# One decoder layer on one core: the order of the first round's loads and products, and the chain of the last norm

## The chip, the core and the metric

The kernel runs on one core of a Trainium2 chip. The core has five engines with queues of their own: PE (matmuls; its weight loads are shown as PEld), DVE and ACT (elementwise work), POOL (GpSimd) and SP, which here only issues DMAs. ACT and POOL can issue DMAs too. The metric is the device time of one execution in microseconds (us), taken as the median of several runs.

## What is computed

The reference is one layer of a decoder trunk in float32 for 256 tokens behind 16 meta tokens, with a width of 2048:

```python
h = jnp.concatenate([meta, x], axis=1)
h = h + hybrid_mixer(rmsnorm(h, norm_mix_g[l]), w_in[l], ...)
h = h + squared_relu_mlp(rmsnorm(h, norm_mlp_g[l]), w_ff1[l], w_ff2[l])
return rmsnorm(h, final_norm_g)[:, N_META:]
```

The mixer projects the normalised input with `w_in` to the operands of a forgetting attention (8 heads) and of a gated linear attention (4 heads), projects both results, gates them and sums them. The MLP is 2048 to 8192 to 2048. What matters here are the two ends: the first products of `w_in` with the input, and the last norm, `rmsnorm(h, final_norm_g)`, with the store of the output.

## The kernel before

**Layout.** Everything is held transposed: `h` has 128 partitions, 16 tiles (`KT`) of 128 channels, 272 tokens, and three columns of gains. A weight block ("chunk") is 2048 x 128, that is 16 tiles of 128 x 128. Each matmul operand is split into a high and a low part (`hi`, `lo`): ACT casts (`whi`), DVE subtracts (`wlo`); the input `x` is split in the same way, with the gain applied. A product is hi x hi, hi x lo and lo x hi. Raw weights, high parts and low parts have five buffers each (`raw`, `whi`, `wlo`). In the main stream SP loads half a chunk (512 KB, line 118), ACT casts it (line 120), DVE makes the low part (line 121), and PE multiplies (lines 136 and 137, or 153 to 155 where all 272 tokens are wanted).

**Order.** The program is written for all engines in one order; a planner that simulates a timeline then sets the order of instructions on each engine (`schedule_with_timeline_sim`). What the planner sets is fixed: an engine does not pass an instruction that waits. `tc.issue_after(ins)` puts what is written in its block behind `ins` on the engine of `ins`.

**First round (lines 259 to 346).** The first seven chunks are not done one after the other but together, so that PE can start before a whole chunk is there. There are eight stages; stage s brings channel tiles k = 2s and 2s+1 of all seven chunks, as one load for chunks 0 to 3 (`wa`, 512 KB) and one for chunks 4 to 6 (`wb`, 384 KB). Stage 0 alone comes in four loads, one for each tile and group. Each chunk accumulates in a PSUM bank of its own (`first_ps`). For each k PE does the high products of all chunks (lines 330, 332, 333) and then the low ones (lines 337, 339). `h` is loaded by line 284: tiles 0 and 1 from ACT's queue, and 2-3, 4-7, 8-15 from SP's queue, between the loads of stages 0, 1 and 2. Lines 317 and 318 make `x`; `square(q)` (lines 288, 290) squares four tiles of `h` for the first norm and is written behind stages 2 to 5. Constants (`cons`), the small columns of `w_in` (`wsm`) and `w_alpha2` follow on SP's queue. Behind the round the seven banks are read out (`total`, lines 162 and 165), the squares are summed over channels by PE (line 208), and PE multiplies the small columns (lines 153 to 155, tile `psa`); it needs a bank that one `total` has set free.

**End (lines 829 to 887).** The last four blocks of `w_ff2` (`NL`) are done in another order: the low products of all 256 tokens first (line 835), and then the high products for tokens 0 to 127 (`half(0, ...)`) and for tokens 128 to 255 (`half(P, ...)`, line 844). Behind each block of a half ACT copies one part of the bank (line 847), DVE adds both to `h` (lines 848, 849), ACT squares (line 851) and applies the gain (line 852), and POOL adds the squares of all but the last block to `acc` (line 854). `root_of` sums the squares over channels on PE (lines 862, 863) and takes the inverse root (`fast_root`, lines 766 to 774: DVE, ACT's square root, a reciprocal, and one Newton step). `spread` puts the roots on a diagonal (line 216, DVE) and has PE spread them over all partitions (line 219). `finish` multiplies `h` and stores it: tokens 0 to 127 on POOL from a copy `r_half` (line 881) with stores from SP's queue, tokens 128 to 255 on DVE straight from PSUM with stores from ACT's queue (lines 871, 872). `finish0`, which does this for the first half, is written behind the third of the second half's four blocks.

Of the kernel before, what the change touches and what calls it, by code (L numbers as in the profile page):

```python
# [16 lines left out]
P = 128  # L17
# [48 lines left out]
def trunk(ctx: ExitStack, tc: tile.TileContext, hT, w_small, w_all, consts, w_alpha2, out):  # L66
# [198 lines left out]
    def first_weights(c0, n, k0):  # L265
# [6 lines left out]
        def load(k, nk):  # L272
            nc.sync.dma_start(r[:, :, k : k + nk, :],
                              w_all[c0 : c0 + n, :, (k0 + k) * P : (k0 + k + nk) * P].rearrange("c p (k m) -> p c k m", m=P))
# [19 lines left out]
    def load_stage(s):  # L294
        stages[s] = [first_weights(c0, n, 2 * s) for c0, n in ((0, 4), (4, 3))]
        for k in range(2) if s == 0 else (0,):
            for hi, lo, load, cut in stages[s]:
                load(k, 1 if s == 0 else 2)

    load_h(nc.scalar, 0, 1)  # L300
    load_h(nc.scalar, 1, 1)
    for _ in range(5):
        nc.tensor.matmul(warm[:, 0:NT], ones[:, 0:P], ones[:, 0:NT], start=True, stop=True)
    load_stage(0)
    load_h(nc.sync, 2, 2)
    load_stage(1)
    load_h(nc.sync, 4, 4)
    load_stage(2)
    load_h(nc.sync, 8, 8)
    nc.sync.dma_start(cons, consts)  # L310
    for s in range(KT // 2):
        if s not in stages:
            load_stage(s)
        wa, wb = stages[s]
        for kk in range(2):
            k = 2 * s + kk
            nc.scalar.activation(x[:, k, 0, :], h[:, k, 0:NA], AF.Identity, scale=gain(0, k))
            nc.vector.scalar_tensor_tensor(x[:, k, 1, :], h[:, k, 0:NA], gain(0, k),
                                           x[:, k, 0, :].bitcast(F32), op0=ALU.mult, op1=ALU.subtract)
            for hi, lo, load, cut in (wa, wb):  # L320
                if s == 0:
                    cut(kk, 1)
                elif kk == 0:
                    cut(0, 2)
            at = [(w[0][:, c, kk, :], w[1][:, c, kk, :]) for w, n in ((wa, 4), (wb, 3)) for c in range(n)]
            st, sp = k == 0, k == KT - 1
            for c, (hi, lo) in enumerate(at):
                ps = first_ps[c]
                if c < NF - 1:
                    nc.tensor.matmul(ps, hi, x[:, k, :, NM:NA], start=st, stop=False)  # L330
                else:
                    nc.tensor.matmul(ps[:, 0:NA], hi, x[:, k, 0, :], start=st, stop=False)
                    nc.tensor.matmul(ps[:, 0:NA], hi, x[:, k, 1, :], start=False, stop=False)
            for c, (hi, lo) in enumerate(at):
                ps = first_ps[c]
                if c < NF - 1:
                    nc.tensor.matmul(ps[:, 0:NT], lo, x[:, k, 0, NM:NA], start=False, stop=sp)  # L337
                else:
                    nc.tensor.matmul(ps[:, 0:NA], lo, x[:, k, 0, :], start=False, stop=sp)
        if s in (2, 3, 4, 5):  # L340
            square(s - 2)
    chunk[0] = NF
    nc.sync.dma_start(wsm, w_small)
    nc.sync.dma_start(wa2[0:16], w_alpha2)
# [419 lines left out]
    def fast_root(sums, n):  # L764
# [7 lines left out]
        nc.vector.tensor_tensor(r, y, y, op=ALU.mult)  # L772
        nc.vector.scalar_tensor_tensor(r, r, -0.5, v, op0=ALU.mult, op1=ALU.mult)
        nc.vector.scalar_tensor_tensor(y, r, 1.5, y, op0=ALU.add, op1=ALU.mult)
        return y
# [63 lines left out]
    def half(t0, between):  # L839

        tok = slice(t0, t0 + P)
        for n, (j, w, ps) in enumerate(ends):
            for k in range(KT):
                nc.tensor.matmul(ps[:, NT:], w(k)[0], a[:, k, :, tok], start=(k == 0), stop=(k == KT - 1))  # L844
            between[n]()
            b = tmp.tile([P, P], F32, tag="evb", name=nm("evb"))
            nc.scalar.copy(b, ps[:, NT + P :])
            nc.vector.tensor_tensor(ht[:, j, tok], ps[:, NT : NT + P], ht[:, j, tok], op=ALU.add)
            nc.vector.tensor_tensor(ht[:, j, tok], ht[:, j, tok], b, op=ALU.add)
            sq = gat.tile([P, P], F32, tag="sq", name=nm("sq"))  # L850
            nc.scalar.activation(sq, ht[:, j, tok], AF.Square)
            nc.scalar.activation(ht[:, j, tok], ht[:, j, tok], AF.Identity, scale=gain(2, j))
            if n < NL - 1:
                nc.gpsimd.tensor_tensor(acc[:, tok], acc[:, tok], sq, op=ALU.add)
        return sq
# [4 lines left out]
    def root_of(i, sq):  # L860
        tok = slice(P * i, P * (i + 1))
        nc.tensor.matmul(pn[i][:, P : P + 1], acc[:, tok], ones[:, 0:1], start=True, stop=False)
        nc.tensor.matmul(pn[i][:, P : P + 1], sq, ones[:, 0:1], start=False, stop=True)
        box[i] = fast_root(pn[i][:, P : P + 1], 1)

    def finish(i, r, pieces):
        tok = slice(P * i, P * (i + 1))
        j0 = 0
        for n, eng in pieces:
            o = ht[:, j0 : j0 + n, tok]  # L870
            eng.tensor_tensor(o, o, r[:, 0:P].unsqueeze(1).to_broadcast([P, n, P]), op=ALU.mult)
            (nc.sync if i == 0 else nc.scalar).dma_start(out[i][:, j0 : j0 + n, :], o)
            j0 += n

    v, p, none = nc.vector, nc.gpsimd, lambda: None
    sq = half(0, [none] * NL)

    def finish0():
        r = gat.tile([P, P], F32, tag="r", name="r_half", bufs=1)
        spread(pn[0], box[0], (0,), P)  # L880
        nc.scalar.copy(r, pn[0][:, 0:P])
        finish(0, r, ((2, p), (2, p), (4, p), (4, p), (4, p)))

    sq = half(P, [lambda: root_of(0, sq)] + [none] * (NL - 3) + [finish0, none])
    root_of(1, sq)
    spread(pn[1], box[1], (0,), P)
    finish(1, pn[1], ((2, v), (2, v), (4, v), (4, v), (4, v)))
# [60 lines left out]
```

## Time and profile before

| | us |
|---|---|
| median of three runs | 1633.47 |
| lowest, highest | 1631.92, 1634.26 |
| the profiled execution's own time | 1630.68 |
| its span in the profile | 1629.0 |
| PE busy in the span | 1609.0 |

The span runs from the first to the last instruction of the profiled execution; 1.68 us of its own time lie around it. PE's busy time is the sum of its matmuls, which are pipelined, and their ends are modelled; here it is used to find the places where PE stands still. A row of a timeline gives start, duration, engine, line, operation, written tile, read tiles, shapes and count; behind it in brackets stand the idle time of the engine just before and what ended it. A row of the chain of waits gives start, duration, engine, tile and line; the chain is followed back from the last instruction.

### The profile page before, as it was taken

How to read it: one execution, taken by the hardware profiler on the slowest of the kernel's cores; microseconds unless marked ns; L12 is line 12 of the kernel's file. 1: busy time of each engine (PE TensorE's matmuls, PEld its weight loads, DVE VectorE, ACT ScalarE, POOL GpSimd, SP SyncE). 2: the span in 40 equal slices, each digit the busy share in tenths (PEclk: the TensorE clock that was granted, in tenths of full speed). 3: DMA queues.
4: the chain of work that ended last, by engine and by line, in shares of the span. 5: the costliest groups of instructions: out<-in, count | busy, mean ns of one | idle time of the engine just before them, and what ended most of it. 6: DMA issues, size and time to landing. Idle time of an engine off the chain costs nothing.

```text
span 1629.0 us, 25617 instructions
## 1 busy us (share of the span) xinstructions
PE 1609.0 (99%) x9996; PEld 1447.2 (89%) x9996; DVE 1033.8 (63%) x1591; ACT 788.3 (48%) x1217; POOL 93.5 (6%) x146
## 2 busy tenths in 40 slices
PE   8999999999999999999999999999999999999997
PEld 7999999999998888888888888888888888888886
DVE  6767657476665555555677776566655676567655
ACT  6555444454445444444555544444444444444553
POOL 1000000010000000000011000000000000000022
PEclk9999999999999999999999999999999999999998
DMA  9444555455555555565555556565566565565552
GB/s 296 137 150 158 159 167 161 164 186 160 161 157 169 191 185 190 186 191 187 188 189 188 185 189 189 187 191 186 181 196 190 188 187 188 188 190 187 190 189 73
DMA packets 90266, 292.97 MB, mean 180 GB/s; under 512 B 9096, under 2 KB 21648, under 8 KB 89888
## 3 DMA queue, kind: packets, MB, share of 16 engines
q1 hardware_dynamic: 87552, 288.88, 55.8%
q8 instruction: 78, 1.28, 0.3%
q10 hardware_dynamic: 2416, 1.33, 0.3%
q0 software_dynamic: 176, 1.12, 0.2%
q14 instruction: 44, 0.36, 0.1%
HBM read 289.19 MB, written 2.11 MB: 179 GB/s over the span
## 4 chain that ended last, share of the span: by engine, by line
PE 97%; DMA 1%; DVE 1%; ACT 0%; issue 0%; SPq 0%; DVEq 0%; ACTq 0%
PE ps L136 50%; PE ps L137 26%; PE psa L155 5%; PE psa L154 5%; PE psa L153 5%; PE ps L844 1%; PE ps L330 1%; DMA h<-hT_dram 1%; PE pa L492 1%; PE ps L835 0%; PE ps L337 0%; PE po L556 0%; DMA raw<-w_all_dram 0%; PE pz L390 0%; PE po L557 0%; PE pq L653 0%
## 5 line engine op out<-in xcount | busy, mean ns | idle before, releaser
L121 DVE TENSOR_TENSOR wlo<-raw,whi 128x1024 fp32r<-128x1024 f32 x522 | 639.9, 1226 | 500.7 <-ACT whi L120 498.9
L120 ACT CAST whi<-raw 128x1024 fp32r<-128x1024 f32 x522 | 548.0, 1050 | 747.5 <-PE ps L136 505.0
L136 PE MATMUL ps<-x,whi 128*128 128x512 f32 x1952 | 685.9, 394 | 0.0
L137 PE MATMUL ps<-x,wlo 128*128 128x256 f32 x1952 | 548.6, 281 | 0.0
L136 PEld LDWEIGHTS ps<-x,whi 128*128 128x128 f32 x1952 | 366.6, 188 | 82.8
L137 PEld LDWEIGHTS ps<-x,wlo 128*128 128x128 f32 x1952 | 367.6, 188 | 0.0
L136 PE MATMUL ps<-a,whi 128*128 128x512 f32 x960 | 335.8, 395 | 0.0
L137 PE MATMUL ps<-a,wlo 128*128 128x256 f32 x960 | 270.0, 282 | 0.0
L136 PEld LDWEIGHTS ps<-a,whi 128*128 128x128 f32 x960 | 180.2, 188 | 40.7
L153 PE MATMUL psa<-x,whi 128*128 128x272 f32 x640 | 186.7, 292 | 2.1 <-DVE ri L196 2.1
L155 PE MATMUL psa<-x,whi 128*128 128x272 f32 x640 | 185.9, 290 | 0.0
L154 PE MATMUL psa<-x,wlo 128*128 128x272 f32 x640 | 184.6, 288 | 0.0
L137 PEld LDWEIGHTS ps<-a,wlo 128*128 128x128 f32 x960 | 181.7, 189 | 0.3
L153 PEld LDWEIGHTS psa<-x,whi 128*128 128x128 f32 x640 | 121.3, 190 | 2.8 <-issue 2.1
L154 PEld LDWEIGHTS psa<-x,wlo 128*128 128x128 f32 x640 | 120.6, 188 | 0.2
L155 PEld LDWEIGHTS psa<-x,whi 128*128 128x128 f32 x640 | 120.3, 188 | 0.1
L136 PE MATMUL ps<-og,whi 128*128 128x512 f32 x256 | 89.9, 393 | 0.0
L136 PE MATMUL ps<-y,whi 128*128 128x512 f32 x256 | 89.1, 392 | 0.0
L756 POOL TENSOR_TENSOR acc<-acc,hsq 128x256 f32<-128x256 f32 x26 | 28.5, 1096 | 774.8 <-ACT hsq L755 774.8
L137 PE MATMUL ps<-y,wlo 128*128 128x256 f32 x256 | 71.8, 281 | 0.0
L137 PE MATMUL ps<-og,wlo 128*128 128x256 f32 x256 | 71.8, 281 | 0.0
L165 DVE TENSOR_TENSOR evt<-ps,evb 128x256 f32<-128x256 f32 x158 | 66.0, 418 | 0.0
(262 smaller groups left out, 1384.9 us busy)
## 6 DMA issues: line engine op xcount, KB each, us to landing
raw<-w_all_dram SPq DMA_DIRECT2D x537, 512.0 KB, 3.9
raw<-w_all_dram SPq DMA_DIRECT2D x7, 384.0 KB, 6.3
h<-hT_dram SPq DMA_DIRECT2D x1, 1100.0 KB, 9.9
negc<-fdram POOLq DMA_DIRECT2D x1, 1088.0 KB, 5.9
out_dram<-h SPq DMA_DIRECT2D x3, 256.0 KB, 2.6
out_dram<-h ACTq DMA_DIRECT2D x3, 256.0 KB, 3.1
h<-hT_dram SPq DMA_DIRECT2D x1, 550.0 KB, 7.3
raw<-w_all_dram SPq DMA_DIRECT2D x2, 256.0 KB, 4.5
```

Source lines behind the costliest of these rows:

```text
L120: nc.scalar.copy(hi[:, k, :], r)
L121: nc.vector.tensor_tensor(lo[:, k, :], r, hi[:, k, :].bitcast(F32), op=ALU.subtract)
L136: nc.tensor.matmul(ps, hi, x, start=first, stop=False)
L137: nc.tensor.matmul(ps[:, 0:NT], lo, x[:, 0, :], start=False, stop=last)
L153: nc.tensor.matmul(ps[:, 0:n], hi, x[:, k, 0, :], start=(k == 0), stop=False)
L154: nc.tensor.matmul(ps[:, 0:n], lo, x[:, k, 0, :], start=False, stop=False)
L155: nc.tensor.matmul(ps[:, 0:n], hi, x[:, k, 1, :], start=False, stop=(k == KT - 1))
L165: nc.vector.tensor_tensor(t, ps[:, 0:NT], b, op=ALU.add)
L330: nc.tensor.matmul(ps, hi, x[:, k, :, NM:NA], start=st, stop=False)
L492: nc.tensor.matmul(dst, k[:, a, :], q[:, a, :], start=(a == 0), stop=(a == 1))
L756: nc.gpsimd.tensor_tensor(acc, acc, sq, op=ALU.add)
L844: nc.tensor.matmul(ps[:, NT:], w(k)[0], a[:, k, :, tok], start=(k == 0), stop=(k == KT - 1))
```

## The change

First round: the loads of `h` all go to SP's queue, two tiles ahead of each stage's weights (one tile at a time in stage 0). Three stages are loaded ahead; in the loop, stage s+3 is loaded, with its `h` behind the first of its two weight loads. `cons`, `wsm` and `w_alpha2` go behind the last weight load of the round. The squares are written behind stages 2, 4, 6 and 7. In the last stage PE finishes one chunk after the other: for each chunk both k, each with its high and low product.

End: both halves of a bank are added to `h` by DVE straight from PSUM, without ACT's copy. POOL adds the squares of two blocks of a half only; the other two are summed by PE. The Newton step has three DVE instructions as before, each with one tensor operand and scalars. ACT makes the diagonal. The first half's `finish0` is put into the second half's last block, ahead of its k = 4, and the matmuls from k = 4 on are put behind its spreading matmul. The second half's stores alternate between ACT's and SP's queue, with pieces of 2, 4, 4, 4 and 2 tiles.

```diff
         def load(k, nk):
-            nc.sync.dma_start(r[:, :, k : k + nk, :],
+            return nc.sync.dma_start(r[:, :, k : k + nk, :],
...
-    def load_stage(s):
-        stages[s] = [first_weights(c0, n, 2 * s) for c0, n in ((0, 4), (4, 3))]
-        for k in range(2) if s == 0 else (0,):
-            for hi, lo, load, cut in stages[s]:
-                load(k, 1 if s == 0 else 2)
-
-    load_h(nc.scalar, 0, 1)
-    load_h(nc.scalar, 1, 1)
+    def load_stage(s, part):
+        c0, n = ((0, 4), (4, 3))[part]
+        w = first_weights(c0, n, 2 * s)
+        stages.setdefault(s, []).append(w)
+        return w[2](0, 2) if s else w[2]
+
+    load_a, load_b = load_stage(0, 0), load_stage(0, 1)
+    for k in range(2):
+        load_h(nc.sync, k, 1)
+        load_a(k, 1)
+        load_b(k, 1)
     for _ in range(5):
         nc.tensor.matmul(warm[:, 0:NT], ones[:, 0:P], ones[:, 0:NT], start=True, stop=True)
-    load_stage(0)
-    load_h(nc.sync, 2, 2)
-    load_stage(1)
-    load_h(nc.sync, 4, 4)
-    load_stage(2)
-    load_h(nc.sync, 8, 8)
-    nc.sync.dma_start(cons, consts)
+    for s in range(1, 3):
+        load_h(nc.sync, 2 * s, 2)
+        load_stage(s, 0)
+        load_stage(s, 1)
     for s in range(KT // 2):
-        if s not in stages:
-            load_stage(s)
+        if s + 3 < KT // 2:
+            with tc.issue_after(load_stage(s + 3, 0).ins):
+                load_h(nc.sync, 2 * s + 6, 2)
+            last = load_stage(s + 3, 1).ins
...
+        if s < KT // 2 - 1:
+            order = [(c, 2 * s + kk, part) for kk in range(2) for part in range(2) for c in range(NF)]
+        else:
+            order = [(c, 2 * s + kk, part) for c in range(NF) for kk in range(2) for part in range(2)]
+        for o in order:
+            products(*o)
+        if s in (2, 4, 6, 7):
+            square((2, 4, 6, 7).index(s))
     chunk[0] = NF
-    nc.sync.dma_start(wsm, w_small)
-    nc.sync.dma_start(wa2[0:16], w_alpha2)
+    with tc.issue_after(last):
+        nc.sync.dma_start(cons, consts)
+        nc.sync.dma_start(wsm, w_small)
+        nc.sync.dma_start(wa2[0:16], w_alpha2)
...
-        nc.vector.tensor_tensor(r, y, y, op=ALU.mult)
-        nc.vector.scalar_tensor_tensor(r, r, -0.5, v, op0=ALU.mult, op1=ALU.mult)
-        nc.vector.scalar_tensor_tensor(y, r, 1.5, y, op0=ALU.add, op1=ALU.mult)
-        return y
+        nc.vector.tensor_scalar(r, y, y, v, op0=ALU.mult, op1=ALU.mult)
+        nc.vector.tensor_scalar(r, r, -0.5, 1.5, op0=ALU.mult, op1=ALU.add)
+        nc.vector.tensor_scalar(q, r, y, None, op0=ALU.mult)
+        return q
...
+                if within and n == NL - 1 and k == 4:
+                    ahead = within()
+                elif not (within and n == NL - 1 and k > 4):
+                    ahead = None
+                with tc.issue_after(ahead) if ahead else nullcontext():
+                    nc.tensor.matmul(ps[:, NT:], w(k)[0], a[:, k, :, tok], start=(k == 0), stop=(k == KT - 1))
             between[n]()
-            b = tmp.tile([P, P], F32, tag="evb", name=nm("evb"))
-            nc.scalar.copy(b, ps[:, NT + P :])
-            nc.vector.tensor_tensor(ht[:, j, tok], ps[:, NT : NT + P], ht[:, j, tok], op=ALU.add)
-            nc.vector.tensor_tensor(ht[:, j, tok], ht[:, j, tok], b, op=ALU.add)
+            for t in (ps[:, NT : NT + P], ps[:, NT + P :]):
+                nc.vector.tensor_tensor(ht[:, j, tok], t, ht[:, j, tok], op=ALU.add)
...
-            if n < NL - 1:
+            if n < NL - 2:
                 nc.gpsimd.tensor_tensor(acc[:, tok], acc[:, tok], sq, op=ALU.add)
-        return sq
+            else:
+                sqs.append(sq)
+        return sqs
...
+        parts = [acc[:, tok], *sqs]
+        for n, part in enumerate(parts):
+            nc.tensor.matmul(pn[i][:, P : P + 1], part, ones[:, 0:1], start=(n == 0), stop=(n == len(parts) - 1))
...
+    def row(i):
+        d = gat.tile([P, P], F32, tag="d", name=nm("d"))
+        nc.scalar.activation(d, ident, AF.Identity, scale=box[i])
+        last = nc.tensor.matmul(pn[i][:, 0:P], ones[:, 0:P], d, start=True, stop=True)
+        r = gat.tile([P, P], F32, tag="r", name=nm("r_half"))
+        nc.scalar.copy(r, pn[i][:, 0:P])
+        return r, last.ins
 
     def finish0():
...
+        r, last = row(0)
+        finish(0, [(j, n, p, r, nc.sync) for j, n in ((0, 2), (2, 2), (4, 4), (8, 4), (12, 4))])
+        return last
+
+    sqs1 = half(P, [lambda: root_of(0, sqs)] + [none] * (NL - 1), finish0)
+    root_of(1, sqs1)
+    row(1)
+    finish(1, [(j, n, v, pn[1], q) for j, n, q in ((0, 2, nc.scalar), (2, 4, nc.sync), (6, 4, nc.scalar),
+                                                  (10, 4, nc.sync), (14, 2, nc.scalar))])
```

More of the change, by code (lines that the diff above doesn't have):

```diff
@@ L1 @@
-from contextlib import ExitStack
+from contextlib import ExitStack, nullcontext
 import concourse.bass as bass
@@ L324, in trunk @@
                     cut(0, 2)
[L325 to L333, printed above, removed]
@@ L875, in trunk @@
     v, p, none = nc.vector, nc.gpsimd, lambda: None
-    sq = half(0, [none] * NL)
-    def finish0():
[L879 to L887, printed above, removed]
+    sqs = half(0, [none] * NL)
```

39 lines of the change are left out of this document (20 added, 19 removed).

## The prediction

> **What bounds the kernel now.** I read the page first, then the rows of waits, then the timelines of the places where PE waits, and last the chain of waits at the end.
>
> ```profile
> PE 1609.0 (99%) x9996; PEld 1447.2 (89%) x9996; DVE 1033.8 (63%) x1591; ACT 788.3 (48%) x1217; POOL 93.5 (6%) x146
> ```
>
> PE is busy for 1609.0 of a span of 1629.0 us, so a change that takes no matmul away can win at most some 20 us, at the places where PE stands still. The timelines of the first 54 us show them:
>
> ```profile
> 1.28 3.87 PE L303 MATMUL warm<-ones 128*128 128x256 f32 x10 [1.28 <-DVE ones L188]
> ...
> 6.63 1.67 PE L330 MATMUL ps<-x,whi 128*128 128x512 f32 x6 [1.48 <-DVE x L318]
> ...
> 8.20 0.94 ACT L317 ACTIVATE x<-h 128x272 fp32r<-128x272 f32 x2 [0.22 <-DMA h<-hT_dram]
> ...
> 10.05 1.76 ACT L278 CAST whi<-raw 128x1024 fp32r<-128x1024 f32 x2
> ...
> 11.70 1.56 PE L330 MATMUL ps<-x,whi 128*128 128x512 f32 x6
> ...
> 16.41 0.94 ACT L317 ACTIVATE x<-h 128x272 fp32r<-128x272 f32 x2 [0.47 <-DMA h<-hT_dram]
> ...
> 21.74 4.18 ACT L278 CAST whi<-raw 128x768 fp32r<-128x768 f32 x5
> ...
> 22.61 0.73 PE L330 MATMUL ps<-x,whi 128*128 128x512 f32 x2 [2.94 <-ACT whi L278]
> ...
> 35.43 1.56 PE L330 MATMUL ps<-x,whi 128*128 128x512 f32 x6
> ...
> 37.91 1.56 PE L330 MATMUL ps<-x,whi 128*128 128x512 f32 x6
> ...
> 50.20 0.29 PE L339 MATMUL ps<-x,wlo 128*128 128x272 f32 x1
> ...
> 52.56 0.42 DVE L165 TENSOR_TENSOR evt<-ps,evb 128x256 f32<-128x256 f32 x1
> ...
> 53.13 0.37 PE L153 MATMUL psa<-x,whi 128*128 128x272 f32 x1 [2.08 <-DVE ri L196]
> ```
>
> One k of the round takes PE 2.48 us (35.43 to 37.91), 16 take 39.7. The round runs from 6.63 to 50.3, 43.7: it loses 4.0 inside. The large wait is 2.94 us at 22.61, for a cast that ACT begins at 21.74. ACT was late because `x` and squares stood ahead of that cast in its order, and these had waited for the load of `h` tiles 8 to 15 (16.41). Ahead of the round PE waits 1.48; behind it 2.08, because DVE reads out the first bank only at 52.56, when the last product is done. With the 1.28 before the first warm-up product these make 8 of the 20 us. The other twelve lie behind the last product, at 1615.37:
>
> ```profile
> 1611.36 4.01 PE ps L844 x33
> ...
> 1615.39 0.27 ACT evb L847
> ...
> 1615.69 0.30 DVE h L848
> ...
> 1616.02 0.78 DVE h L849
> ...
> 1616.88 0.32 ACT sq L851
> ...
> 1617.24 0.40 PE pn L863 x2
> ...
> 1617.66 0.17 DVE rv L766
> ...
> 1617.85 0.21 ACT rq L768
> ...
> 1618.09 0.17 DVE ry L770
> ...
> 1618.29 0.19 DVE rr L772
> ...
> 1618.50 1.11 DVE rr L773
> ...
> 1619.63 1.10 DVE ry L774
> ...
> 1620.76 0.30 DVE diag L216
> ...
> 1621.10 0.81 PE pn L219 x2
> ...
> 1621.94 0.42 DVE h L871
> ```
> ```profile
> 1613.02 0.46 POOL L854 TENSOR_TENSOR acc<-acc,sq 128x128 f32<-128x128 f32 x1 [1.88 <-ACT sq L851]
> 1613.04 0.53 DVE L216 TENSOR_SCALAR diag<-cons,ry 128x128 f32<-128x128 f32 x1
> ...
> 1615.19 0.38 PE L219 MATMUL pn<-diag,ones 128*128 128x128 f32 x2
> ...
> 1615.96 4.76 POOL L871 TENSOR_TENSOR h<-h,r_half 128x256 f32<-128x256 f32 x5 [0.59 <-ACT r_half L881]
> ```
>
> Lines 773 and 774 work on one column and take 1.1 us each, line 849 takes 0.78. All three read two tensors from SBUF, and all three run while POOL does its five multiplications (1615.96 to 1620.72). The reciprocal (ry, 1618.09), also SBUF to SBUF but with one tensor, takes 0.17 there, and rv, which reads PSUM, 0.17. So a two-tensor operation of DVE waits for POOL's current instruction.
>
> **The change, part by part.** All sums are against the profiled execution (1630.68, span 1629.0). The median of the three runs is 2.8 higher; I take the same difference off it.
>
> *First round.* Two bounds. PE's first product cannot come before the five warm-up products end at 5.15: at most 1.48 is won. Stage 1 gives the sharper one. In both versions the 1171 KB of stage 0 (896 of weights, two tiles of `h` of 137.5) and 275 KB of `h` go ahead of its first weights; that `h` landed by 8.20. The next 512 KB take 1.4 us at the rate of that time:
>
> ```profile
> GB/s 0 82 292 335 314 363 361 398 365 426 406 341 352 366 278 316 347 192 0 198 304 247 331 294 371 382 391 303 267 240 237 164 218 52 0 67 276 52 33 215
> ```
>
> (slices of 1.35 us, some 360 GB/s there), so they land at 9.6; today's cast starts at 10.05, straight behind a square that moves away. Cast and start add 0.9: PE begins stage 1 at 10.5, not 11.70. From there the loads bring a stage (1171 KB) in 3.3 us and PE needs 4.96, so the lead grows.
>
> ```profile
> 6.60:50.30 43.70, 40.56 (x240) 35.45 (x241) 29.50 (x41) 27.07 (x41) 3.75 (x4) 1.00 0.83 276
> ```
>
> Over the round DVE (29.50) and ACT (27.07) are busy for 68% and 62% of the time, today crowded into its first half by the early `h`; spread over the stages they keep up with PE. I expect no further wait but 0.1 for low parts. The round ends at 10.5 + 14 x 2.48 + 0.1 = 45.3: **-5.0**. Nothing won (the planner again puts `x` and squares ahead of casts) is one end, -5.5 (1.48 + 4.0) the other. I choose near the good end, as the named load is split and each piece now lies ahead of its own stage.
>
> SP's order: the first `h` moves from ACT's queue to SP's, and the later tiles go behind loads that wait for a free `raw` buffer; who waits for it is `x`, priced among the rivals. `cons`, `wsm` and `w_alpha2` go behind the last load. That one goes out when stage 5's first load has been cut, which needs a `whi` buffer that PE leaves with stage 2 (10.5 + 2 x 4.96 = 20.4): at about 22. The first user (the small columns' cast) needs a buffer of stage 5, free at 35, so these loads have 13 us. The main stream's weights queue behind them on SP; PE needs those only behind the round.
>
> *Last stage by chunk.* The same matmuls in another order: no cost. The first bank is complete 6/7 of 4.96, 4.2 us, ahead of the end, and its sum takes DVE 0.42 (52.56) behind a shorter copy on ACT. Both have that time, so PE goes straight on: **-2.1**. With the sum placed behind the casts of the main stream again, 0.
>
> *The end.* T is the end of the last product (1615.37 now). Start to start: without ACT's copy -0.30. The second addition reads PSUM; no row shows such an operation begun inside one of POOL's. I take 0.30 like the first, as the nearest row (rv, from PSUM beside POOL) is not held: -0.48; held as today, 0. The Newton step keeps three instructions but with one tensor each; I take 0.20 each like the reciprocal, -1.86 for two; held, they cost what they do now. The diagonal on ACT costs 0.40 + 0.04, like line 852's gain on the same shape, against 0.34: +0.10.
>
> ```profile
> L852 ACT ACTIVATE h<-h x8: 401/402/405, 1602.1 to 1617.2; 128x128 f32<-128x128 f32 x8
> ```
>
> The spreading product took 0.81 at half the clock, and 0.38 for the first half, at full clock. It had fallen by 1618.75, 3.4 us behind T:
>
> ```profile
> 1618.75:1619.00 0.25, 0.00 (x0) 0.00 (x0) 0.25 (x1) 0.00 (x0) 0.25 (x1) 0.50 0.07 19
> ```
>
> Now it would begin 3.2 behind T, just before: -0.42; 0 if the fall comes earlier. The Trainium skill's "TensorE: Matmul & The Clock Gate" ("What's actually happening") says that the clock is cut after an idle window of about 3.4 us that runs freely. The 3.4 agrees; by the rule T need not be a window's start, the fall comes at T + 3.4 at the earliest and mostly later, and the -0.42 holds for sure, where by the row alone 0.2 us of margin decide and it may be 0.
>
> The sum is -2.96: DVE's multiplication begins at T + 3.6 in place of T + 6.6. But POOL moves less. The first half's spreading now stands 12 products ahead of T (12 x 0.12 = 1.46); a copy of 0.27 follows, and ACT has a square and a gain of the third block in the way (0 to 0.7): POOL begins about T - 0.75, not T + 0.59, and ends at T + 4.0, behind DVE's start. So its last store (256 KB) falls into the second half's.
>
> ```profile
> 1625.00:1625.50 0.50, 0.00 (x0) 0.00 (x0) 0.00 (x0) 0.00 (x0) 0.00 (x0) 0.50 0.99 297
> 1627.00:1627.50 0.50, 0.00 (x0) 0.00 (x0) 0.00 (x0) 0.00 (x0) 0.00 (x0) 0.50 0.43 130
> ```
>
> The stores end near 1627.3 with all queues full at some 290 GB/s: 256 KB more cost 0 to 0.9, I take 0.6. Two queues do not help, since the DMA engines are full. End: **-2.4**; with all that may be held, +0.4, and without the overlap -3.0.
>
> *PE's additions.* One more pair of sums ahead of T: **+0.1**. The wait put before k = 4: the diagonal of the first half must be there at T - 1.7. Today it is done at 1613.57 (T - 1.8), 0.2 of it DVE's wait for POOL. If it is late, PE stalls with 12 products behind it: 0 to 1; I take 0.
>
> **Sum:** -5.0 - 2.1 - 2.4 + 0.1 = -9.4: span 1619.6, 1621.3 for this execution, and 1633.5 - 9.4 = **1624.1** for the median.
>
> **The rivals.** *A. The start gives back.* The planner orders ACT and DVE by its own times, and an order that was wrong by several us made today's 2.94. One of the two gains goes: if the readout of the first bank stays behind the casts, 1626.2; if the first round gains nothing, 1629.1. For: both orders stand in the trace. Against: the cause of each, a late load and a late bank, is taken away.
>
> *B. One-column operations wait for POOL too.* Line 216, one tensor with scalars on 128 columns, took 0.53 beside POOL (1613.04) and 0.30 alone: it ended 0.09 after POOL. If the Newton step did that, its first instruction, at T + 2.1, would wait for the end of POOL's fourth piece and the second for its fifth, T + 4.0; the step ends at T + 4.2 instead of T + 2.7. The spreading then meets the slow clock (+0.4), and the stores' overlap (0.6) goes: +1.3, 1625.4. Against: the reciprocal's 0.17. The Trainium skill's "SBUF — State Buffer" ("SBUF: two separate sides") has it as a lock that a DVE operation takes in a two-port mode or with two SBUF inputs: by the first half of that rule this case could come; the diagonal's 0.53 agrees with it, and no run here shows it for a column.
>
> *C. Only the end is won.* The change doesn't do at the start what it says: both of these waits come back, since the planner's order stands ahead of any load that comes later than it believed. 1633.5 - 2.4 = 1631.1, which counts as no change.
>
> *D. `h` comes too late (slower).* Five `raw` buffers and two loads a stage let a load, its cast (0.84) and its low part (1.0) take 2.5 stages, 12.4 us; a landing above 10.6 us makes each stage wait. Over stages 3 to 7 it outweighs the 9.4 from a landing of 15.3 (1.9 a stage); at 17 it costs 12.8, 1636.9. For: `h` now stands in that queue. Against:
>
> ```profile
> DMA to landing us min/median/max: 3.4/5.4/10.3
> ```
>
> these loads' longest was 10.3, behind 1100 KB of `h`.
>
> **How the numbers follow.** Chances: forecast 0.60, A 0.15, B 0.09, C 0.10, D 0.06. The range goes from the best ends (-5.5, -2.1, -3.0: 1622.9) less the runs' own 1.5 below the median, 1621.4, to A's far end with as little above, 1629.5; that leaves out C and D. A measurement tells 0.2%, 3.3 us, from no change. Faster by more: forecast, A and B, 0.84; the same: C, 0.10; slower: D, 0.06.
>
> **What would show it.** Right: PE's first round without an idle time above 0.5 us and over near 45; line 153 begins within a us of it; lines 848 and 849's successors at 0.3 and the Newton step at 0.16 while POOL runs; spreading at 0.4; some 11.2 us from T to the span's end. Wrong: casts of line 278 that begin behind `x` of later tiles; PE waiting for ACT's diagonal ahead of k = 4; DVE's one-column rows near 1 us; stores that end later than T + 9.7.

## The result, and the profile after

The changed kernel takes 1623.42 us (median of six, 1623.12 to 1623.76), the kernel before 1633.15 in the same comparison (median of six, 1631.92 to 1634.26): 9.7 us less, a ratio of 0.9942 with a 95% interval of 0.9932 to 0.9953. The forecast was 1624.1. The total came out near the forecast; its terms did not, as the profile shows. T is the end of the last product, S the start of DVE's first multiplication behind it.

| us from the span's start | before | after | forecast after |
|---|---|---|---|
| first product | 6.63 | 5.21 | 5.15 or later |
| stage 1 begins | 11.70 | 12.02 | 10.5 |
| the round ends | 50.3 | 46.8 | 45.3 |
| line 153 begins | 53.13 | 47.38 | 46.0 |
| T | 1615.37 | 1610.05 | 1608.4 |
| from T to S | 6.57 | 4.47 | 3.6 |
| from T to the span's end | 13.63 | 11.65 | 11.2 |
| span | 1629.0 | 1621.7 | 1619.6 |
| the profiled execution's own time | 1630.68 | 1623.76 | 1621.3 |

The span became 7.3 shorter: 5.75 up to line 153 and 1.98 behind T, less 0.43 between the two. PE's busy time is the same as before (1609.0), so all of this is idle time of PE. First the page of the changed kernel, then its timeline at the start:

```profile
PE 1609.0 (99%) x10000; PEld 1447.0 (89%) x10000; DVE 1030.6 (64%) x1589; ACT 787.8 (49%) x1212; POOL 92.8 (6%) x144
```
```profile
5.21 1.73 PE L334 MATMUL ps<-x,whi 128*128 128x512 f32 x6
...
9.09 0.94 ACT L320 ACTIVATE x<-h 128x272 fp32r<-128x272 f32 x2 [0.68 <-DMA h<-hT_dram]
...
9.93 1.10 ACT L288 ACTIVATE room<-h 128x1088 f32<-128x1088 f32 x1
...
10.94 1.77 ACT L278 CAST whi<-raw 128x1024 fp32r<-128x1024 f32 x2
...
12.02 1.66 PE L334 MATMUL ps<-x,whi 128*128 128x512 f32 x6 [1.29 <-ACT whi L278]
...
46.79 0.72 PE L208 MATMUL prb<-ones,room 128*128 128x1 f32 x6
47.38 0.37 PE L153 MATMUL psa<-x,whi 128*128 128x272 f32 x1
```

The waits of 1.48, 2.94 and 2.08 us are gone. A new one of 1.29 stands ahead of stage 1: ACT had a square (9.93) ahead of the cast (10.94), and `h` for that stage had landed only at 9.07. From 12.02 on PE does not stand still: 14 x 2.48 = 34.7 leads to 46.8, and a stretch of 26 us in it is 26 us of PE (the row gives the stretch and its length, the busy time and in brackets the number of instructions of PE, PEld, DVE, ACT and POOL, and then the granted clock of PE, the busy share of the DMA engines and GB/s):

```profile
16.00:42.00 26.00, 26.00 (x160) 23.23 (x159) 20.71 (x28) 17.26 (x25) 3.10 (x4) 1.00 0.96 323
```

Line 153 follows the sums of the squares (line 208) with no wait. The timeline of the end:

```profile
1609.01 4.73 POOL L892 TENSOR_TENSOR h<-h,r_half 128x256 f32<-128x256 f32 x5 [1.30 <-ACT r_half L904]
...
1610.08 0.62 DVE L867 TENSOR_TENSOR h<-ps,h 128x128 f32<-128x128 f32 x2 [1.49 <-PE ps L864]
...
1612.20 0.27 DVE L785 TENSOR_SCALAR rr<-ry,rv 128x1 f32<-128x1 f32 x1
1612.51 0.15 DVE L786 TENSOR_SCALAR rr<-rr 128x1 f32<-128x1 f32 x1
1612.70 0.21 DVE L787 TENSOR_SCALAR rq<-rr,ry 128x1 f32<-128x1 f32 x1
1612.94 0.40 ACT L901 ACTIVATE d<-cons,rq 128x128 f32<-128x128 f32 x1 [0.98 <-DVE rq L787]
1613.40 0.80 PE L902 MATMUL pn<-d,ones 128*128 128x128 f32 x2 [1.86 <-ACT d L901]
1614.23 0.27 ACT L904 COPY r_half<-pn 128x128 f32<-128x128 f32 x1 [0.88 <-PE pn L902]
1614.53 1.61 DVE L892 TENSOR_TENSOR h<-h,pn 128x256 f32<-128x256 f32 x3 [1.62 <-ACT r_half L904]
```

All of DVE's steps lie beside POOL's multiplications (1609.01 to 1613.74), and none is held: 0.27, 0.15 and 0.21 where lines 773 and 774 took 1.1 each, and two additions in 0.62 where the second alone took 0.78. Two rows are longer than forecast: the spreading product took 0.80, not 0.4, and ACT's copy `r_half`, which nobody uses in this half, stands between it and DVE's multiplication.

### The profile page after: what moved, and what is told of

Its sections match the earlier page's. It is cut to its first block, busy times and chain, and to the rows that moved or that the text cites. A ratio compares the mean times of both kernels' runs of the same rounds, so it can differ in the third digit from the quotient of the medians.

```text
span 1621.7 us, 25628 instructions
## 1 busy us (share of the span) xinstructions
PE 1609.0 (99%) x10000; PEld 1447.0 (89%) x10000; DVE 1030.6 (64%) x1589; ACT 787.8 (49%) x1212; POOL 92.8 (6%) x144
## 4 chain that ended last, share of the span: by engine, by line
PE 99%; DMA 0%; ACT 0%; DVE 0%; SPq 0%; issue 0%; DVEq 0%; ACTq 0%
PE ps L136 51%; PE ps L137 26%; PE psa L155 5%; PE psa L154 5%; PE psa L153 5%; PE ps L334 1%; PE ps L864 1%; PE ps L339 1%; PE pa L504 1%; PE ps L848 0%; DMA h<-hT_dram 0%; PE po L568 0%; PE pz L402 0%; PE po L569 0%; PE pq L665 0%; PE po L182 0%
```

## The experiments

Times are medians (lowest to highest, number of executions); the ratio is to the kernel before, run on the same chip. The runs below come from four chips, on which the fastest execution of the kernel before took between 1630.44 and 1630.65. The chips thus differ little, but the changed kernel's 1623.42 is from another comparison, and differences of some tenths between the medians of variants are read from the profiles.

| run | us | ratio, 95% interval |
|---|---|---|
| start only | 1625.72 (1625.35 to 1626.21, 4) | 0.9962, 0.9948 to 0.9975 |
| end only | 1631.64 (1629.33 to 1633.18, 10) | 0.9994, 0.9984 to 1.0003 |
| before again | 1632.03 (1630.75 to 1634.60, 8) | 0.9997, 0.9987 to 1.0007 |
| last stage by k again | 1627.32 (1625.99 to 1628.03, 7) | 0.9970, 0.9960 to 0.9981 |
| before, its waits filled | 1630.92 (1630.42 to 1631.47, 11) | 0.9992, 0.9983 to 1.0001 |
| squares behind their casts | 1623.16 (1622.86 to 1623.44, 5) | 0.9946, 0.9933 to 0.9958 |
| first `h` on ACT's queue | 1623.44 (1622.89 to 1623.82, 4) | 0.9946, 0.9932 to 0.9959 |
| no unused copy | 1622.91 (1622.66 to 1623.39, 5) | 0.9944, 0.9932 to 0.9957 |
| Newton step on two tensors | 1624.61 (1624.32 to 1624.87, 4) | 0.9954, 0.9940 to 0.9968 |
| PE kept busy at the end | 1624.35 (1623.11 to 1624.85, 5) | 0.9952, 0.9938 to 0.9965 |
| both small edits | 1622.88 (1622.42 to 1623.86, 5) | 0.9943, 0.9930 to 0.9955 |
| both, and `h` on ACT's queue | 1623.73 (1622.98 to 1624.61, 5) | 0.9948, 0.9935 to 0.9962 |

### The two halves alone, and the kernel before again

Start only has the changed loads, first round and last stage with the end as it was; end only the reverse; the third is the kernel before without an edit.

The main edit of start only, against the changed kernel (the Newton step, DVE's diagonal and the old order of `finish0` come back with it):

```diff
-            for t in (ps[:, NT : NT + P], ps[:, NT + P :]):
-                nc.vector.tensor_tensor(ht[:, j, tok], t, ht[:, j, tok], op=ALU.add)
+            b = tmp.tile([P, P], F32, tag="evb", name=nm("evb"))
+            nc.scalar.copy(b, ps[:, NT + P :])
...
```

> The first round's part alone, with the old end. From the profile after: line 153 begins near 47.4 in place of 53.1, the end takes 13.6 from the last product as before: span about 1623.3, 5.7 less than the profile before. In the medians: 5.7 less if the kernel before is the same in all executions; 7.5 to 8.5 less, and runs within 0.7 us of each other, if its scatter lies in the first round.

> The end's part alone, with the old first round. Line 153 begins as before (53.1 or later); from the last product to the end 11.6 in place of 13.6: 1.6 to 2.1 less in the medians. If the scatter lies in the first round, this kernel's runs scatter by some 2 us like those before.

> The kernel before once more, for the 2.5 us by which its profiled execution (1630.68) was below its median (1633.15). Theory 1: its executions differ in the first round, where the casts stand behind the load of h tiles 8 to 15; then in a slower execution line 153 begins later than 53.13 by what the span is longer than 1629.0, and from line 153 to the end it takes 1575.9 as before. Theory 2: they differ at the end or over the whole span; then line 153 begins at 53.1 again and the rest is longer.

By the profile the halves nearly add up: start only has line 153 at 47.60 and 13.85 from T to the end, end only has 11.67 there, 1.96 less than the kernel before. By the medians they don't, and both expectations were missed: the start alone gained 6.25, against 1631.97 for the kernel before on that chip, where 5.7 or 7.5 to 8.5 were expected; the end alone gained 0.3, where 1.6 to 2.1 were. The end's gain is there and drowns: end only scatters by 3.9 us and the kernel before by 4.2, start only by 0.9. What scatters is in the start that the change removes. The second profile of the kernel before shows it, in stretches of 1 us behind its waits of 3.00 (at 22.48) and 2.08; beside it is one stretch of its first profile:

```profile
22.00:23.00 1.00, 0.52 (x2) 0.48 (x3) 1.00 (x3) 1.00 (x2) 0.00 (x0) 0.94 1.09 344
23.00:24.00 1.00, 1.00 (x4) 0.86 (x4) 1.00 (x3) 1.00 (x2) 0.00 (x0) 0.50 0.74 229
24.00:25.00 1.00, 1.00 (x4) 0.75 (x3) 1.00 (x2) 1.00 (x3) 0.00 (x0) 0.50 0.01 3
...
54.00:55.00 1.00, 1.00 (x5) 1.00 (x6) 0.98 (x6) 0.83 (x3) 0.00 (x0) 0.50 0.94 279
```
```profile
53.87 0.57 PE L153 MATMUL psa<-x,whi 128*128 128x272 f32 x1 [2.08 <-DVE ri L196]
```
```profile
23.00:24.00 1.00, 1.00 (x6) 0.72 (x5) 1.00 (x3) 1.00 (x2) 0.00 (x0) 1.00 0.76 236
```

In the first profile the clock (third number from the right) is 1.00 behind both waits. In the second it is 0.50 for 3.4 us behind each: line 153 comes 0.74 later although the first wait ended 0.13 earlier, and line 153 to T takes 1563.65 instead of 1562.24. The span is 2.1 longer, 1631.1: a part of the scatter lies ahead of line 153 and a part behind it, so neither theory of this run holds alone. The mean granted clock of an execution tells which it was. In 65 executions of the kernel before, over four chips:

| mean granted clock | executions | median us |
|---|---|---|
| 0.997 | 16 | 1630.69 |
| 0.996 | 23 | 1631.70 |
| 0.995 | 17 | 1633.22 |
| 0.994 | 9 | 1634.23 |

0.997 is what the end alone makes: in the first profile the clock is 0.50 from 1618.75 on, for the last 10.25 us, and 10.25 x 0.5 of 1629.0 is 0.0031. Each further fall of 3.4 us takes another 0.001, so the four rows are none, one, two and three falls: the first profile has none and 0.997, the second two and 0.995, and end only two and 0.995. Three is an estimate from these numbers; no profile shows it. Among executions of the same mean clock, end only (medians 1629.66 at 0.997, 1631.77 at 0.995, one execution of 1633.18 at 0.994) lies 1.0 to 1.5 below the kernel before. The profiled execution of the kernel before was one of the 0.997; all six of the changed kernel have 0.997 or 0.998.

### Is it the waits? One brought back, and both filled

Two runs test that. In one, the last stage of the changed kernel goes by k again, which brings the wait ahead of line 153 back. In the other, the kernel before gets products that nobody uses in its two waits, so that PE stands still less while nothing is taken off the path.

Last stage by k again, against the changed kernel:

```diff
-        if s < KT // 2 - 1:
+        if True:
```

> The changed kernel with the last stage in the old order (all chunks for one k, high products first). Theory 1: the readout of the first bank comes behind the round again and line 153 starts 2 us later, 1625.5 in the median. Rival (the earlier loads and squares alone have cleared ACT and DVE there): the wait is 1.0 or less, since only a copy of 0.4 and a sum of 0.4 lie between the last product and line 153.

Before, its waits filled, against the kernel before:

```diff
-                    nc.tensor.matmul(ps[:, 0:NT], lo, x[:, k, 0, NM:NA], start=False, stop=sp)
+                    low = nc.tensor.matmul(ps[:, 0:NT], lo, x[:, k, 0, NM:NA], start=False, stop=sp)
+                    if k == 5 and c == 3:
+                        with tc.issue_after(low.ins):
+                            for _ in range(3):
+                                nc.tensor.matmul(warm[:, 0:NT], ones[:, 0:P], ones[:, 0:NT], start=True, stop=True)
...
+        with tc.issue_after(end.ins):
+            for _ in range(2):
+                nc.tensor.matmul(norm1["ps"][:, 304:512], ones[:, 0:P], ones[:, 0:208], start=True, stop=True)
```

> The kernel before, with products that nobody uses in its two waits: three of 128 x 256 behind the last product ahead of the 2.94 us wait at 22.61, and two of 128 x 208 behind the sums of the squares, ahead of the wait of 2.08 at 53.13. Nothing is taken off the path, so the profiled best case stays. Theory 1 (before scatters by 4 us because its two waits let the clock fall in most executions, and the change wins some 1 to 2.5 us by taking the waits away, beside what the waits themselves cost): the mean granted clock is 0.997 in nearly all executions, no stretch between 22 and 58 us is granted 0.50, the scatter falls under 1.5 us, and the median falls from some 1632.0 to 1630.5 to 1630.9. Theory 2 (the clock of before falls for a reason of its own, or the scatter lies elsewhere): clocks of 0.994 to 0.997 as in before, a median within 0.5 of before's, and a scatter of 3 to 4.

The first, by k again (a row of its timeline, and a stretch behind it):

```profile
49.55 0.36 PE L153 MATMUL psa<-x,whi 128*128 128x272 f32 x1 [2.07 <-DVE ri L196]
```
```profile
51.00:52.00 1.00, 1.00 (x6) 1.00 (x6) 0.93 (x6) 0.18 (x1) 0.00 (x0) 0.50 0.93 320
```

Line 153 comes 2.17 later than in the changed kernel, and from there to T it takes 1565.14 instead of 1562.67, 2.47 more. Of these, 1.5 arise ahead of line 848's first product (1540.56 instead of 1539.05 from line 153), behind the fall of the clock; the other 1.0 is a wait near the end that has another cause (see "PE kept busy at the end"). So the wait costs 2.1 itself and 1.5 through the clock in this execution; the median is 3.9 higher. The second, with the waits filled:

```profile
7.05 2.50 PE L331 MATMUL ps<-x,whi 128*128 128x512 f32 x6 [1.94 <-DVE x L319]
...
21.44 1.46 PE L342 MATMUL warm<-ones 128*128 128x256 f32 x6
23.06 0.73 PE L331 MATMUL ps<-x,whi 128*128 128x512 f32 x2 [0.16 <-ACT whi L279]
```
```profile
8.00:9.00 1.00, 1.00 (x4) 0.74 (x3) 1.00 (x2) 0.80 (x2) 0.00 (x0) 0.50 1.09 350
...
23.00:24.00 1.00, 0.94 (x4) 0.67 (x4) 1.00 (x3) 1.00 (x3) 0.00 (x0) 1.00 0.70 231
...
54.00:55.00 1.00, 1.00 (x11) 1.00 (x10) 0.97 (x5) 0.75 (x3) 0.00 (x0) 1.00 0.74 234
```

The clock stays at 1.00 behind both, though 1.20 of the second wait is left. 9 of 11 executions have 0.997 and the others 0.996, where 4 of 15 of the kernel before beside it have 0.997. The scatter is 1.05 instead of 3.8, and the median is 1.66 lower (1632.58 to 1630.92; the ratio's interval just reaches 1), although PE multiplies more. This is theory 1: the waits let the clock fall, in most executions, and the change wins that too. The profiled execution is one of the 0.996: its clock fell at 7.6, for 3.4 us, behind the wait for `x` ahead of the round, which was not filled and took 1.94 us here (1.48 and 0.55 in the two profiles of the kernel before). The changed kernel has no such wait.

### The start: the square, and SP's queue

The new wait of 1.29 has two causes in the trace: the square ahead of the cast, and loads that land late. The first run puts each square behind its stage's last cast on ACT; the second loads the first two tiles of `h` from ACT's queue again.

Against the changed kernel (in the first, `cut` returns its cast):

```diff
-            square((2, 4, 6, 7).index(s))
+            with tc.issue_after(cast.ins):
+                square((2, 4, 6, 7).index(s))
```
```diff
-        load_h(nc.sync, k, 1)
+        load_h(nc.scalar, k, 1)
```

> The changed kernel with each square put behind the casts of the stage that it is written at, so that ACT casts stage 1 before the first square. Theory 1 (the square's 1.1 us stands in the way): the wait of 1.29 at stage 1 becomes 0.2 to 0.4 and the round ends 0.9 to 1.1 earlier, 1622.4 in the median. Rival (the weights of stage 1 land only then): the cast waits for its load instead, and the time stays within 0.3.

> The changed kernel, but the first two tiles of `h` are loaded from ACT's queue again, as before the change. Theory 1 (in the changed kernel SP's queue alone issues too slowly at the start: 199 and 229 GB/s in the microseconds 4 to 5 and 5 to 6, against 351 and 297 before; two issues less of some 0.5 us each bring stage 1's first weights some 0.9 us earlier): some 300 GB/s in these two microseconds, stage 1's cast able to begin near 9.7 instead of 10.5, and line 153 begins 0.4 to 0.9 us earlier than the 47.38 of the changed kernel if the square does not stand in the way, so a time of some 1622.6 to 1623.0. Theory 2 (the sizes of the rows set the rate, whichever queue issues): the same rate in these microseconds and a time within 0.3 of 1623.4. Theory 3 (ACT's issues, 1.0 us ahead of its first table load, delay the first `x` and casts as before the change): the first product of the round begins near 6.6 instead of 5.2 and up to 1.4 us are lost, 1624.8.

Squares behind casts: the square is gone from in front of the cast, and the cast waits for its load instead:

```profile
10.54 1.95 ACT L278 CAST whi<-raw 128x1024 fp32r<-128x1024 f32 x2 [0.52 <-DMA raw<-w_all_dram]
...
11.64 1.65 PE L335 MATMUL ps<-x,whi 128*128 128x512 f32 x6 [0.15 <-ACT whi L278]
```

Stage 1 begins 0.4 earlier only, and the median moves by 0.26. With `h` on ACT's queue, the rate in the fifth and sixth microsecond (last number); first this run, then the changed kernel, then the kernel before:

```profile
4.00:5.00 1.00, 1.00 (x4) 0.82 (x3) 0.00 (x0) 0.45 (x1) 0.00 (x0) 1.00 1.14 347
5.00:6.00 1.00, 0.91 (x3) 0.19 (x1) 0.80 (x2) 0.81 (x3) 0.00 (x0) 1.00 1.18 293
```
```profile
4.00:5.00 1.00, 1.00 (x4) 0.82 (x3) 0.40 (x2) 0.82 (x2) 0.00 (x0) 1.00 0.98 199
5.00:6.00 1.00, 1.00 (x6) 0.86 (x5) 0.98 (x2) 0.30 (x1) 0.00 (x0) 1.00 0.80 229
```
```profile
4.00:5.00 1.00, 1.00 (x5) 0.69 (x3) 0.00 (x0) 0.18 (x1) 0.00 (x0) 1.00 1.13 351
5.00:6.00 1.00, 0.15 (x1) 0.00 (x0) 0.53 (x1) 0.86 (x2) 0.00 (x0) 1.00 1.20 297
```
```profile
6.36 1.65 PE L334 MATMUL ps<-x,whi 128*128 128x512 f32 x6 [0.45 <-DVE x L321]
...
11.42 1.56 PE L334 MATMUL ps<-x,whi 128*128 128x512 f32 x6
```

The move of `h` to SP's queue is what slows the stream. All 14 profiles say so: the eight with the first `h` on SP's queue have 155 to 199 and 212 to 269 GB/s in these two microseconds, the six with it on ACT's 336 to 358 and 293 to 314. With ACT's queue the rate is back and stage 1 begins at 11.42 without a wait (the last fence is this run's timeline). But the first product comes at 6.36, since `x` now waits behind a cast on ACT. What SP's queue wins at the first product it loses at stage 1, and ACT's the other way round: line 153 came at 46.70 in this profile, yet the median (1623.44) is that of the changed kernel. The rate is theory 1's, the late first product theory 3's, and together they give theory 2's time. Both the square and the queue are in the trace, and neither alone is worth more than some tenths.

### The end: the copy, the Newton step, the clock

No unused copy, against the changed kernel:

```diff
-    def row(i):
+    def row(i, copied=True):
...
+        if not copied:
+            return
         r = gat.tile([P, P], F32, tag="r", name=nm("r_half"))
...
-    row(1)
+    row(1, False)
```

> The changed kernel without the second half's copy of the spread row (line 904), which nothing reads. Theory 1 (DVE's first multiplication waits for that copy, 0.30): it starts 0.3 sooner behind the spreading product, and the span ends 0.2 to 0.4 sooner. Rival (the stores fill the DMA engines anyway): DVE starts 0.3 sooner but the end comes at the same time, within 0.1.

```profile
1613.44 0.79 PE L902 MATMUL pn<-d,ones 128*128 128x128 f32 x2 [1.86 <-ACT d L901]
1614.27 2.21 DVE L892 TENSOR_TENSOR h<-h,pn 128x256 f32<-128x256 f32 x4 [1.32 <-PE pn L902]
```

DVE's multiplication now follows the product itself: S is T + 4.17 instead of 4.47, and T to the end takes 11.3 instead of 11.65. The median is 0.5 less. In the changed kernel the program lets DVE wait for ACT here, though both only read the bank. The Trainium skill's "PSUM — Partial Sum Buffer" (its table of terms) says why such accesses are kept apart: two engines on the same bank and the same quarter of its partitions at once collide, "reads against reads included"; no run here tried that.

Newton step on two tensors, against the changed kernel:

```diff
-        nc.vector.tensor_scalar(r, y, y, v, op0=ALU.mult, op1=ALU.mult)
-        nc.vector.tensor_scalar(r, r, -0.5, 1.5, op0=ALU.mult, op1=ALU.add)
-        nc.vector.tensor_scalar(q, r, y, None, op0=ALU.mult)
+        nc.vector.tensor_tensor(r, y, y, op=ALU.mult)
+        nc.vector.scalar_tensor_tensor(r, r, -0.5, v, op0=ALU.mult, op1=ALU.mult)
+        nc.vector.scalar_tensor_tensor(q, r, 1.5, y, op0=ALU.add, op1=ALU.mult)
```

> The changed kernel with the old Newton step: one instruction with twice the same tensor, two that read two tensors from SBUF. Theory 1 (such an operation waits for POOL's current instruction): the three take until the end of POOL's running pieces, the two last 0.5 to 1.2 each, and the span ends 0.8 to 1.6 later. Rival (the old 1.1 us came from something else than POOL): 0.16 each, and the time is the same or 0.1 less.

```profile
1609.74 4.06 POOL L892 TENSOR_TENSOR h<-h,r_half 128x256 f32<-128x256 f32 x4
...
1612.73 1.09 DVE L786 SCALAR_TENSOR_TENSOR rr<-rr,rv 128x1 f32<-128x1 f32 x1
1613.86 0.16 DVE L787 SCALAR_TENSOR_TENSOR rq<-rr,ry 128x1 f32<-128x1 f32 x1
```

The same form takes 1.09 beside POOL, ending as POOL's last piece ends at 1613.80, and 0.16 right behind it. In start only, which has the old end, both rows take 0.16 for the first half of the tokens, where POOL is idle (1607.12 and 1607.32). S moves to T + 5.49, the median by 1.2. So operations with two SBUF tensors wait for POOL and these with one do not, on a single column too; the "half of that rule" by which rival B could come did not act on a column.

PE kept busy at the end (two products that nobody uses, behind the last sum, which is `end` in the lines), against the changed kernel:

```diff
+        if i == 1:
+            with tc.issue_after(end.ins):
+                for _ in range(2):
+                    nc.tensor.matmul(pn[0][:, NT:512], ones[:, 0:P], ones[:, 0:NT], start=True, stop=True)
```

> The changed kernel with two more fp32 products of 256 columns on PE, of ones, into an unused part of a bank, between the second half's sums and its spreading product. Theory 1 (the clock falls while PE is idle, 2.7 us behind the last product): the clock stays at 1.00 until the spreading product, which takes 0.40 in place of 0.81, and the span ends 0.3 to 0.4 sooner. Rival (the few products don't count as work, or the clock falls at a fixed time): 0.81 again; or the added products end behind 3.3 us and delay the spreading, and the span is 0 to 0.5 longer.

```profile
1590.74 2.34 PE L848 MATMUL ps<-a,wlo 128*128 128x256 f32 x16 [0.51 <-DVE h L773]
...
1614.28 0.49 PE L906 MATMUL pn<-d,ones 128*128 128x128 f32 x2 [0.89 <-ACT d L905]
```

The spreading product took 0.49 and S was T + 4.16, but the run is slower, by a wait of 0.51 at 1590.74, far ahead of the two products: line 848's first stretch up to line 864's first product takes 6.59 instead of 5.60. In the trace the wait goes back to the last load of weights. It was issued at 1582.5, as in the changed kernel (1582.6), but landed 6.3 us later instead of 4.9, and ACT casts it ahead of the copy (line 772) that DVE's line 773 waits for, and PE for that. In last stage by k again that load also took 6.3, and PE waited 0.49 at the same place, so the two products are not the cause; why the load was late stays open. The price of the clock isn't settled by this run either: the same 0.49 came without added products with the squares behind their casts and with `h` on ACT's queue, where the product also began 3.3 to 3.4 behind T. Of the eight profiles that reach it there without added products, two show 0.49 and six 0.79 to 0.80.

### Both small edits

The first run has the edits of "squares behind their casts" and "no unused copy" together; the second has that of "first `h` on ACT's queue" as well:

```diff
-            square((2, 4, 6, 7).index(s))
+            with tc.issue_after(cast.ins):
+                square((2, 4, 6, 7).index(s))
...
-    row(1)
+    row(1, False)
```

> The changed kernel with two edits that each won a little alone: the squares are put behind their stage's last cast on ACT (0.3 alone), and the second half's copy `r_half`, which nothing uses, is left out (0.3 to 0.5 alone). Theory 1 (the two lie at the two ends and add): line 153 near 47.0, DVE's last multiplication at T + 3.9 to 4.2, a median of 1622.5 to 1622.8. Theory 2 (the spreading product meets the lower clock again, or the planner orders something else anew): no better than 1622.9, the better of the two alone.

> The kernel of the two small edits (squares behind their casts, no unused copy), and the first two tiles of `h` from ACT's queue. If the queue is what makes stage 1's weights land late (theory 1 of the run with `h` on ACT's queue), stage 1 begins near 10.8 instead of 11.6 and the median is some 0.8 below the kernel of the two edits: 1621.8. If the rows' sizes set the rate (theory 2): the same as that kernel within 0.3. If ACT's issues delay the first product (theory 3): up to 1.4 above it.

Together they give 1622.88, no better than the copy alone (1622.91): 0.5 below the changed kernel, with intervals that overlap widely. In its profile stage 1's load landed late:

```profile
11.41 1.92 ACT L278 CAST whi<-raw 128x1024 fp32r<-128x1024 f32 x2 [0.54 <-DMA raw<-w_all_dram]
...
12.51 0.73 PE L335 MATMUL ps<-x,whi 128*128 128x512 f32 x2 [1.89 <-ACT whi L278]
```

The same load, in the same order, let its cast begin at 10.54 with the squares alone and at 11.41 here: executions differ by 0.9 in when a load lands. With ACT's queue added, the first product came at 7.00 (a wait of 1.49 for `x`), 0.64 later than with that edit alone, and the median is 1623.73. This is what theory 3 expected, and the gain of theory 1 is gone. Of the differences at the start among these kernels only their size, below one microsecond, is settled.

## Why the prediction was right in total and wrong in its terms

**First round, forecast -5.0, measured -3.5.** The first product came 1.42 earlier, but the step that failed is stage 1's start: "so they land at 9.6", at the rate of the time before, and a cast "straight behind a square that moves away". The square did not move away (9.93), and the load landed late (10.54 and 11.41 in the two profiles shown, whose casts wait for nothing else), because the rate was not that of before: SP now issues all loads, and the stream ran at 199 and 229 GB/s where it had run at 351 and 297. The forecast counted `h` on SP's queue only as a risk for late `x`. From stage 1 on it held: no wait, 2.48 a tile. Whether the order of `h` or the later squares removed the wait of 2.94 no run separates; they were changed together.

**Wait behind the round, forecast -2.1, measured -2.2** (from the round's end to line 153, 2.8 before and 0.6 after). The mechanism was right: with k again as the inner order it comes back at 2.07.

**PE's additions, forecast +0.1, measured +0.43** from line 153 to T; 0.36 of it is in the timeline of the changed kernel, a second pair of sums (1603.48 to 1603.70) and the first half's spreading, now ahead of T (0.14):

```profile
1603.48 0.36 PE L884 MATMUL pn<-ones,sq 128*128 128x1 f32 x2
...
1603.70 1.42 PE L864 MATMUL ps<-a,whi_last 128*128 128x256 f32 x10
...
1608.24 0.38 PE L902 MATMUL pn<-d,ones 128*128 128x128 f32 x2
1608.38 1.66 PE L864 MATMUL ps<-a,whi_last 128*128 128x256 f32 x12
```

**End, forecast -2.4, measured -1.98.** The adds were right within 0.1 and the Newton step within 0.15 (0.74 for its three instructions where 0.61 was forecast). Three sizes were not. The copy was missed, a term put at nothing without a reason: 0.30. The spreading product was to meet the full clock: 0.81 in the chain of waits instead of 0.38, +0.43. And the stores' overlap, +0.6, did not come: from S to the end it took 7.17, and 7.06 before, since POOL was done (1613.74) 0.8 before the late S. The Newton step and the unused copy have runs of their own; the other terms of the end are read from rows, and the queues of the stores were not tested alone. As for the clock, the changed kernel's stretches show it falling at 1612.75:

```profile
1612.50:1612.75 0.25, 0.00 (x0) 0.00 (x0) 0.20 (x2) 0.00 (x0) 0.25 (x2) 1.00 0.97 295
1612.75:1613.00 0.25, 0.00 (x0) 0.00 (x0) 0.16 (x1) 0.06 (x1) 0.25 (x1) 0.50 0.98 297
```

That is T + 2.7. The forecast's use of the Trainium skill's "TensorE: Matmul & The Clock Gate", that the fall comes at T + 3.4 at the earliest, is refuted by it; the margin of 0.2 us that "the row alone" gave was the better warning. In the 14 profiles the fall comes between T + 2.3 (end only) and T + 5.4 (start only).

**The step from the profiled execution to the median** failed most: "the median of the three runs is 2.8 higher; I take the same difference off it". The 2.8 was no constant; it came from the falls of the clock behind the waits that the change removes. The changed kernel's profiled execution lies 0.34 above its median, the one before 2.47 below the median of its six: that is 2.8 more. So 9.7 is 6.9 between the two profiled executions (7.3 in the span, less 0.4 that lies around it) and 2.8 from there to the medians, where the forecast had 9.4 and nothing. Two errors of nearly the same size, 2.5 and 2.8, cancelled: that the total came within 0.7 us was luck.

**The rivals.** A came neither way: both waits went. B is refuted by the rows beside POOL. C did not come; the end alone, which is its case, took 1631.64 against its 1631.1. D did not come: between 12.02 and 46.79 PE waits for no `x`. The range's upper end, 1629.5, is 0.4 above A's 1629.1, though the runs lay up to 0.8 above the median; nothing depended on it.

## What to carry to other kernels

A wait of PE of 2 to 3 us can cost more than its length, here 0.9 to 1.5 us more, and not in every execution: compare the mean granted clocks of several executions before the profiled one is taken for the median. When loads are moved to one queue, work out when each is issued and lands there, and don't carry over the old rate. On a chain at the end, look for everything that reads the same PSUM bank, unused copies too, and keep operations with two SBUF tensors away from a busy POOL.

## What was not expected of the hardware

- The clock fell to 0.50 behind waits of only 1.94 to 3.02 us, for 3.4 us each time, and a fall behind the two larger waits cost 0.9 to 1.5 us; in 49 of 65 executions of the kernel before, the mean clock was below what the end alone makes. Other waits of up to 2.08 us, and one of 2.94, were followed by no fall.
- Behind the last dense product it fell after 2.7 us in the changed kernel, although short products lie in between, and in other executions not within 3.3.
- A load's landing varied by 0.9 us at the start and by 1.4 us near the end between profiles that issued it at nearly the same time.
- A one-column operation with two scalars read from SBUF (line 785) took 0.27 us, beside an idle POOL as well as beside a busy one, where the one with constants (line 786) took 0.15.
